# A branch projection by seven half-size products, with its right factors formed one stage earlier

## The chip, the cores and the metric

The kernel runs on one core of a Trainium2 chip. The metric is the device time of one execution in microseconds (us). The profile names the engines PE (TensorE matmul), PEld (its weight loads), DVE (VectorE), ACT (ScalarE), POOL (GpSimd) and SP (SyncE, which here only issues DMAs). L751 is line 751 of the kernel.

## The reference

One encoder layer is applied to two request groups, 256 and 512 tokens, together 768 tokens of width 1024. Three token mixers (an S5 scan, differential attention, cross-attention) each give an output of 1024 channels. What matters here is how they are merged:

```python
branches = jnp.stack([s5_out, diff_out.astype(x.dtype), mem_out.astype(x.dtype)], axis=2)
br = jnp.einsum('blnc,ncd->blnd', branches, w_branch[li])
gates = jax.nn.sigmoid((gl + b_gate[li]).astype(F32)).reshape(Bsz, L, N_BRANCH, D_MODEL)
merged = jnp.sum(gates * br.astype(F32), axis=2).astype(x.dtype)
x = x + merged @ w_out[li]
h2 = rmsnorm(x, ffn_norm_g[li])
g, up = jnp.split(h2 @ w_gate_up[li], 2, axis=-1)
x = x + (jax.nn.silu(g) * up) @ w_down[li]
```

So each branch is a product of a 1024x1024 weight with 1024x768 activations, scaled by a sigmoid gate and summed.

## The kernel before

Activations of all 768 tokens lie with channels on the partitions: a tile of 128 x 8 x 768 holds all 1024 channels. A float32 product is done as three products (`mm3`, L748 to L753): each operand is split into a high part (an ACT copy that rounds) and a low part (a DVE subtraction), and high x high, high x low and low x high are added up in PSUM. `split_evac` (L739) makes such a pair from a source.

Weights stream through `WStream` (L504): SP loads half chunks of 128x1024 into three raw buffers, ACT writes the high part (L595) and DVE the low part (L601) into four buffer pairs. `get()` (L613) hands out a chunk of 256 output columns and first has the splits of the next chunk issued. For the gate and up weights of the FFN the kind is "w": POOL forms four sums of the chunk's quarters (`_split_w`, L561; L572, L573, L577, L579), and ACT and DVE split seven factors of 128x512 (`_factor`, L547; L557, L558). `block` (L1458) then multiplies by Strassen's method in Winograd's form: seven products with half the inner size, half the output rows and half the tokens (384) instead of eight, each four k-steps of `mm3`. The right factors (B11 to B22, T1 to T4) are made once by `right_factors` (L1693).

The three branches go in the order 2, then the GLU of the S5 path, then 0, then 1 (the last branch). `branch` (L1505) takes four chunks of 256 output columns; for each of the two row blocks m of a chunk it loads the gate row from DRAM on POOL's queue (L1513, two buffers), takes its tanh on ACT (L1514), and for the segments of 256 and 512 tokens does eight k-steps of `mm3` into one of three PSUM banks (`psd`). `merge` scales by the gate on DVE (L1520, reads PSUM) and adds to `merged` on DVE (L1523). In the last branch the finished row is split at once into MG (ACT L1554, DVE L1555), the left operand of the output projection. The input of the last branch, `br_scr`, is loaded on POOL's queue row by row (`load_pair`, L1561, two buffers shared under the tag `brr`) and split during branch 0 into the pair Xd (L742, L743). The residual rows x1 are loaded on POOL's queue in the second chunk of branch 0 (L1616). After the last branch come the output projection (`out_rows`, L1633, five PSUM banks), which adds into x1 (L1643), the norm, and the FFN.

Tiles of a pool rotate: a new tile waits until the one that held its buffer has been read. Within an engine, instructions are issued in an order that the framework fixes at build time from its own timeline; `keep_in_program_order` pins an instruction behind everything written before it on its engine.

Of the kernel before, what the change touches and what calls it, by code (L numbers as in the profile page):

```python
# [8 lines left out]
F32 = mybir.dt.float32  # L9
F32R = mybir.dt.float32r  # L10
# [493 lines left out]
class WStream:  # L504
# [53 lines left out]
        self.nc.vector.tensor_tensor(out=f(lo), in0=src, in1=f(hi).bitcast(F32), op=ALU.subtract)  # L558
        self.parts.setdefault(i, {})[key] = f(hi), f(lo)

    def _split_w(self, i, h):  # L561
        gt = self.nc.gpsimd.tensor_tensor
        add, sub = ALU.add, ALU.subtract
        view = lambda t: t.rearrange("p (k m c) -> p m k c", k=4, m=2)
        new = lambda k: self.sums.tile([128, 4, 128], F32, name=f"ws{i}{k}", tag="ws")
        if h == 0:
            return
        a1, a2 = view(self.raw.pop(2 * i)), view(self.raw.pop(2 * i + 1))
        A11, A21, A12, A22 = a1[:, 0], a1[:, 1], a2[:, 0], a2[:, 1]
        self._factor(i, "A11", A11)  # L570
        s1, s2, s3, s4 = (new(k) for k in range(4))
        gt(out=s1, in0=A21, in1=A22, op=add)  # L572
        gt(out=s2, in0=s1, in1=A11, op=sub)  # L573
        self._factor(i, "A12", A12)
        self._factor(i, "S2", s2)
        self._factor(i, "S1", s1)
        gt(out=s3, in0=A11, in1=A21, op=sub)  # L577
        self._factor(i, "S3", s3)
        gt(out=s4, in0=A12, in1=s2, op=sub)  # L579
        self._factor(i, "S4", s4)  # L580
        self._factor(i, "A22", A22)

    def _split(self):
        i, h = divmod(self.n_split, 2)
        self.n_split += 1
        kind = self.src[i][3]
        if kind == "w":
            return self._split_w(i, h)
# [6 lines left out]
        self.nc.scalar.activation(hi, r, AF.Copy)  # L595
# [5 lines left out]
        self.sub.tensor_tensor(out=lo, in0=r, in1=hi.bitcast(F32), op=ALU.subtract)  # L601
# [11 lines left out]
    def get(self, ahead=True):  # L613
        i = self.next
        self.next += 1
        if ahead:
            self.ahead(i + 1)
        _, kk, cols, kind = self.src[i]
        p = self.parts.pop(i)
        if kind == "w":  # L620
            return p
        k2 = kk // 2
        at = lambda t, k, c0, n: t[:, cols * (k % k2) + c0 : cols * (k % k2) + c0 + n]
        return lambda k, c0, n: tuple(at(t, k, c0, n) for t in p[k // k2])


def hybrid_block(ctx, tc, A, outs, consts):
# [20 lines left out]
    def uid(s):  # L648
        cnt[0] += 1
        return f"{s}_{cnt[0]}"  # L650
# [97 lines left out]
    def mm3(ps, wh, wl, xh, xl, start, stop, more=False):  # L748

        kw = {"skip_group_check": True} if more else {}  # L750
        pe.matmul(ps, wh, xh, start=start, stop=False, **kw)  # L751
        pe.matmul(ps, wh, xl, start=False, stop=False, **kw)  # L752
        pe.matmul(ps, wl, xh, start=False, stop=stop, **kw)  # L753
# [740 lines left out]
    with ExitStack() as c5:  # L1494
# [7 lines left out]
        def pair(pool, nm):  # L1502
            return tuple(pool.tile([128, 8, TOK], F32R, name=uid(nm + w), tag="X" + w) for w in ("hi", "lo"))

        def branch(n_, X, first=False, MG=None, tick=None, hook=None):  # L1505
            for c in range(4):
                if hook:
                    hook(c)
                w = W.get()

                def gate(m):
                    g = gtp.tile([128, TOK], F32, name=uid("glr"), tag="glr")
                    gp.dma_start(g, gl_scr[8 * n_ + 2 * c + m])  # L1513
                    act.activation(g, g, AF.Tanh, scale=0.5)  # L1514
                    return g

                def merge(m, g, ps, c0, n):
                    M = 2 * c + m
                    dst = merged[:, M, c0 : c0 + n] if first else g[:, c0 : c0 + n]
                    v.scalar_tensor_tensor(out=dst, in0=g[:, c0 : c0 + n], scalar=1.0, in1=ps[:, 0:n],  # L1520
                                           op0=add, op1=mul)
                    if not first:
                        v.tensor_tensor(out=merged[:, M, c0 : c0 + n], in0=merged[:, M, c0 : c0 + n],  # L1523
                                        in1=dst, op=add)

                if first and c == 0:

                    gs = [gate(m) for m in range(2)]
                    between = lambda: tick(1.0 / 8)
                    for m in range(2):  # L1530
                        ps = psd("br")
                        dense_fm(ps, w, m, X, 0, 256, between=between)
                        merge(m, gs[m], ps, 0, 256)
                        between()
                    pss = [psd("br") for _ in range(2)]
                    for o in (0, 256):
                        for m in range(2):
                            dense_fm(pss[m][:, o : o + 256], w, m, X, 256 + o, 256, between=between)
                            between()
                    for m in range(2):  # L1540
                        merge(m, gs[m], pss[m], 256, 512)
                    continue
                for m in range(2):
                    M = 2 * c + m
                    g = gate(m)
                    for sg, (c0, n) in enumerate(SEGS):
                        ps = psd("br")
                        between = tick and (lambda: tick((1.0 + sg) / 8))
                        dense_fm(ps, w, m, X, c0, n, between=between)
                        merge(m, g, ps, c0, n)  # L1550
                        if tick:
                            between()
                    if MG:
                        act.activation(MG[0][:, M], merged[:, M], AF.Copy, scale=0.5)  # L1554
                        v.scalar_tensor_tensor(out=MG[1][:, M], in0=merged[:, M], scalar=0.5,  # L1555
                                               in1=MG[0][:, M].bitcast(F32), op0=mul, op1=sub)

# [14 lines left out]
        def tail(c):  # L1572
            if c != 3:
                return
            dat.drain()
            dctx.close()
            xp = x1ctx.enter_context(tc.tile_pool(name="x1", bufs=1))
            L["x1"] = [xp.tile([128, 1024], F32, name=f"x1_{t}") for t in range(TILES)]
# [6 lines left out]
        x1, XB, Z = L["x1"], L["XB"], L["Z"]  # L1585
        S = rows_pair("s5o")
        for c in range(4):
            w = W.get()
# [7 lines left out]
            for m in range(2):  # L1596
# [352 lines left out]
```

## Time and profile before

| what | us |
|---|---|
| median of 3 runs (lowest, highest) | 1745.99 (1744.87, 1746.82) |
| the profiled execution | 1746.11 |
| its span | 1744.3 |
| branch 0, first to last product | 1052.9 to 1119.9 |
| last branch, first to last product | 1120.1 to 1186.6 |
| output projection, first to last product | 1186.9 to 1253.7 |
| FFN gate blocks by seven products, first to last start | 1291.7 to 1568 |

Times in the trace count from the start of the span. A matmul's recorded duration is longer than its distance from the next one, since matmuls are pipelined, so rates are taken from starts. A group of instructions is shown as line, engine, operation, output<-input, shapes and count, then durations or busy time, and the idle time of the engine just before with what ended it. The granted TensorE clock was 1.00 in the stretches looked at.

### The profile page before, as it was taken

How to read it: one execution, taken by the hardware profiler on the slowest of the kernel's cores; microseconds unless marked ns; L12 is line 12 of the kernel's file. 1: busy time of each engine (PE TensorE's matmuls, PEld its weight loads, DVE VectorE, ACT ScalarE, POOL GpSimd, SP SyncE). 2: the span in 40 equal slices, each digit the busy share in tenths (PEclk: the TensorE clock that was granted, in tenths of full speed). 3: DMA queues.
4: the chain of work that ended last, by engine and by line, in shares of the span. 5: the costliest groups of instructions: out<-in, count | busy, mean ns of one | idle time of the engine just before them, and what ended most of it. 6: DMA issues, size and time to landing. Idle time of an engine off the chain costs nothing.

```text
span 1744.3 us, 29493 instructions
## 1 busy us (share of the span) xinstructions
PE 1731.5 (99%) x11236; PEld 1606.4 (92%) x11236; DVE 1262.6 (72%) x2353; ACT 889.4 (51%) x1868; POOL 270.1 (15%) x288
## 2 busy tenths in 40 slices
PE   9999999999999999999999999999999999999999
PEld 9999988999999999999989888888889999998887
DVE  7665749699999778887886445453598777776775
ACT  7444543776767346877775434232343333334443
POOL 0000000000000100111010002000036555541130
PEclk9999999999999999999999999999999999999999
DMA  8222736755566453745653437331312323238973
GB/s 271 74 85 91 125 120 134 187 126 141 145 158 159 122 145 93 169 91 155 169 160 106 133 116 247 118 118 61 90 62 91 109 91 109 91 110 290 252 158 96
DMA packets 209214, 234.11 MB, mean 134 GB/s; under 512 B 57832, under 2 KB 173296, under 8 KB 209072
## 3 DMA queue, kind: packets, MB, share of 16 engines
q1 hardware_dynamic: 182160, 167.49, 31.9%
q0 software_dynamic: 17440, 58.34, 15.5%
q10 hardware_dynamic: 9472, 6.39, 1.3%
q8 instruction: 89, 1.46, 0.4%
q14 instruction: 53, 0.43, 0.1%
HBM read 165.78 MB, written 41.22 MB: 119 GB/s over the span
## 4 chain that ended last, share of the span: by engine, by line
PE 96%; DVE 1%; ACT 1%; DMA 1%; issue 0%; SPq 0%; ACTq 0%; DVEq 0%
PE gl L751 4%; PE gl L753 4%; PE gl L752 4%; PE br L751 4%; PE br L752 4%; PE br L753 4%; PE gate L751 3%; PE gate L752 3%; PE up L752 3%; PE gate L753 3%; PE up L751 3%; PE up L753 3%; PE dn L753 3%; PE dn L751 3%; PE dn L752 3%; PE qk L751 3%
## 5 line engine op out<-in xcount | busy, mean ns | idle before, releaser
L595 ACT ACTIVATE wh<-wr 128x1024 fp32r<-128x1024 f32 x124 | 140.4, 1133 | 62.6 <-PE br L752 27.8
L601 DVE TENSOR_TENSOR wl<-wr,wh 128x1024 fp32r<-128x1024 f32 x82 | 108.5, 1324 | 80.8 <-ACT wh L595 79.0
L751 PE MATMUL gl<-H,wh 128*128 128x256 f32 (+1 forms) x384 | 132.2, 344 | 0.0
L753 PE MATMUL gl<-H,wl 128*128 128x256 f32 (+1 forms) x384 | 129.0, 336 | 0.0
L752 PE MATMUL gl<-H,wh 128*128 128x256 f32 (+1 forms) x384 | 128.7, 335 | 0.0
L599 POOL DMA_DIRECT2D wl<-wr x42 | 36.6, 872 | 506.1 <-ACT wl L598 486.8
L751 PE MATMUL qk<-wh,H 128*128 128x256 f32 x384 | 108.1, 282 | 0.0
L752 PE MATMUL qk<-wl,H 128*128 128x256 f32 x384 | 107.8, 281 | 0.0
L753 PE MATMUL qk<-wh,H 128*128 128x256 f32 x384 | 107.1, 279 | 0.0
L752 PE MATMUL dn<-wld,dxh 128*128 128x512 f32 x231 | 89.6, 389 | 0.0
L751 PE MATMUL dn<-whd,dxh 128*128 128x512 f32 x231 | 89.6, 389 | 0.0
L753 PE MATMUL dn<-whd,dxl 128*128 128x512 f32 x231 | 88.9, 389 | 0.0
L753 PEld LDWEIGHTS gl<-H,wl 128*128 128x128 f32 x384 | 72.0, 188 | 8.1
L752 PEld LDWEIGHTS gl<-H,wh 128*128 128x128 f32 x384 | 72.3, 188 | 7.2
L751 PEld LDWEIGHTS gl<-H,wh 128*128 128x128 f32 x384 | 72.3, 188 | 6.8
L557 ACT ACTIVATE wh_S<-ws 128x512 fp32r<-128x512 f32 x70 | 41.1, 625 | 65.2 <-PE up L752 36.8
L753 PEld LDWEIGHTS qk<-wh,H 128*128 128x128 f32 x384 | 72.4, 188 | 0.6
L751 PEld LDWEIGHTS qk<-wh,H 128*128 128x128 f32 x384 | 72.4, 188 | 0.6
L752 PEld LDWEIGHTS qk<-wl,H 128*128 128x128 f32 x384 | 72.3, 188 | 0.5
L558 DVE TENSOR_TENSOR wl_S<-ws,wh_S 128x512 fp32r<-128x512 f32 x70 | 57.9, 851 | 15.9 <-ACT wh_S L557 15.9
L1292 DVE TENSOR_REDUCE nm<-sc 128x1 f32<-128x512 f32 (+1 forms) x96 | 56.6, 596 | 17.6 <-PE sc L1287 16.8
L1294 ACT ACTIVATE p<-sc,nm 128x512 f32<-128x512 f32 (+1 forms) x96 | 58.8, 615 | 14.1 <-DVE nm L1292 13.6
(477 smaller groups left out, 6004.2 us busy)
## 6 DMA issues: line engine op xcount, KB each, us to landing
wr<-in_w_in_dram SPq DMA_DIRECT2D x48, 512.0 KB, 4.9
wr<-in_w_gate_up_dram SPq DMA_DIRECT2D x44, 512.0 KB, 3.6
wl<-wr POOLq DMA_DIRECT2D x42, 512.0 KB, 5.4
wr<-in_w_branch_dram SPq DMA_DIRECT2D x24, 512.0 KB, 4.8
glr<-gl_scr POOLq DMA_DIRECT2D x24, 384.0 KB, 4.0
hid_scr<-fa SPq DMA_DIRECT2D x11, 768.0 KB, 6.5
wr<-in_w_mem_kv_dram SPq DMA_DIRECT2D x16, 512.0 KB, 4.2
wr<-in_w_in_dram SPq DMA_DIRECT2D x32, 256.0 KB, 3.8
```

The source lines that it names most:

```text
L557: self.nc.scalar.activation(f(hi), src, AF.Copy)
L558: self.nc.vector.tensor_tensor(out=f(lo), in0=src, in1=f(hi).bitcast(F32), op=ALU.subtract)
L595: self.nc.scalar.activation(hi, r, AF.Copy)
L599: self.nc.gpsimd.dma_start(lo, r.bitcast(F32R), accum_op=ALU.add)
L601: self.sub.tensor_tensor(out=lo, in0=r, in1=hi.bitcast(F32), op=ALU.subtract)
L751: pe.matmul(ps, wh, xh, start=start, stop=False, **kw)
L752: pe.matmul(ps, wh, xl, start=False, stop=False, **kw)
L753: pe.matmul(ps, wl, xh, start=False, stop=stop, **kw)
L1292: v.tensor_reduce(out=nm[:, m : m + 1], in_=ps, axis=AX.X, op=ALU.max, negate=True)
L1294: act.activation(pm[:, 0:n], ps, AF.Exp, bias=nm[:, m : m + 1], accum_out=s1s[:, tt : tt + 1] if m == 0 else s2)
```

## The change

The last branch is done by seven products a chunk, with the weight kind "w2": as "w", with one buffer fewer for the sums (the fourth is formed in place of the second). Before branch 0 is written, the four row pairs of `br_scr` (rows k and k+4) are loaded and the right factors formed: B11, B22, B21, T1, T3 and T2 are split at once (ACT and DVE), their differences are taken on DVE, and T4 is kept unsplit. Six of the factors lie in the buffers of the Z pair and in the memory of x1, whose loads therefore move behind the last branch; T4's pair lies in the last two rows of MG, which is why the last chunk does A22 T4 before S4 B22.

In a chunk, products add onto banks already in use: S2 T2 and S3 T3 onto the bank of A11 B11 (`chain`), S4 B22 onto that of S1 T1 (`p5`), each after ACT has copied out what the bank held (c11, c12, c22). Four additions from PSUM are left on DVE. Both gate rows of a chunk are loaded at its start, with the two buffers as before. `merge` scales a whole row of 768 in SBUF on DVE, adds it to `merged` on POOL for the first row of the chunk and on DVE for the second, and splits it into MG.

```diff
-    def _split_w(self, i, h):
+    def _split_w(self, i, h, inplace=False):
...
-        s1, s2, s3, s4 = (new(k) for k in range(4))
+        s1, s2 = new(0), new(1)
+        if not inplace:
+            s3, s4 = new(2), new(3)
         gt(out=s1, in0=A21, in1=A22, op=add)
         gt(out=s2, in0=s1, in1=A11, op=sub)
         self._factor(i, "A12", A12)
         self._factor(i, "S2", s2)
         self._factor(i, "S1", s1)
+        if inplace:
+            s3, s4 = new(2), s2
         gt(out=s3, in0=A11, in1=A21, op=sub)
         self._factor(i, "S3", s3)
         gt(out=s4, in0=A12, in1=s2, op=sub)
...
-            W.add(cols(nme, 256 * c), 8, 256)
+            W.add(cols(nme, 256 * c), 8, 256, "w2" if nme == "w_branch1" else None)
...
-        Xd = pair(XB, "xd")
-        load_pair(Xd, br_scr)
-
-        def rows_in(c):
-            if c == 1:
-                for t in range(TILES):
-                    tc.keep_in_program_order(gp.dma_start(x1[t], xs[t]))
-
-        branch(0, S, hook=rows_in)
+        fctx = c5.enter_context(ExitStack())
+        W.sums = fctx.enter_context(tc.tile_pool(name="wsumb", bufs=2))
+        t4p = fctx.enter_context(tc.tile_pool(name="t4raw", bufs=1))
+        t4 = t4p.tile([128, 4, HT], F32, name="t4")
...
+        for k in range(4):
+            r0, r1 = (stg.tile([128, TOK], F32, name=uid("brr"), tag="brr") for _ in range(2))
+            gp.dma_start(r0, br_scr[k])
+            gp.dma_start(r1, br_scr[k + 4])
+            (b11, b12), (b21, b22) = ((r[:, h1], r[:, h2]) for r in (r0, r1))
+            put = lambda n_, src: split_evac(RB[n_][0][:, k], RB[n_][1][:, k], src)
+            put("B11", b11)
+            put("B22", b22)
+            put("B21", b21)
+            v.tensor_tensor(out=b11, in0=b12, in1=b11, op=sub)
+            v.tensor_tensor(out=b12, in0=b22, in1=b12, op=sub)
+            v.tensor_tensor(out=b22, in0=b22, in1=b11, op=sub)
+            v.tensor_tensor(out=t4[:, k], in0=b21, in1=b22, op=sub)
+            put("T1", b11)
+            put("T3", b12)
+            put("T2", b22)
+
+        branch(0, S)
         MG = rows_pair("mgd", 0)
-        branch(1, Xd, MG=MG)
+        RB["T4"] = tuple(t[:, 6:8].rearrange("p a (b t) -> p (a b) t", b=2) for t in MG)
+
+        def branch7(n_):
+            for c in range(4):
+                w = W.get()
+                if c == 0:
+                    for k in range(4):
+                        split_evac(RB["T4"][0][:, k], RB["T4"][1][:, k], t4[:, k])
+                gs = []
+                for m in range(2):
+                    g = gtp.tile([128, TOK], F32, name=uid("glr"), tag="glr")
+                    gp.dma_start(g, gl_scr[8 * n_ + 2 * c + m])
+                    act.activation(g, g, AF.Tanh, scale=0.5)
+                    gs.append(g)
+                cs = [stg.tile([128, TOK], F32, name=uid("bs"), tag="brr") for _ in range(2)]
+                (c11, c12), (c21, c22) = ((t[:, h1], t[:, h2]) for t in cs)
+                chain = env.psb("brc")[:, 0:HT]
...
+                def plus(o, ps):
+                    v.tensor_tensor(out=o, in0=o, in1=ps, op=add)
+
+                def merge(m):
+                    M = 2 * c + m
+                    v.scalar_tensor_tensor(out=cs[m], in0=gs[m], scalar=1.0, in1=cs[m], op0=add, op1=mul)
+                    (v if m else gp).tensor_tensor(out=merged[:, M], in0=merged[:, M], in1=cs[m], op=add)
+                    act.activation(MG[0][:, M], merged[:, M], AF.Copy, scale=0.5)
+                    v.scalar_tensor_tensor(out=MG[1][:, M], in0=merged[:, M], scalar=0.5,
+                                           in1=MG[0][:, M].bitcast(F32), op0=mul, op1=sub)
+
+                act.activation(c11, prod("A11", "B11", chain), AF.Copy)
+                plus(c11, prod("A12", "B21"))
+                act.activation(c12, prod("S2", "T2", chain, False), AF.Copy)
+                p5 = prod("S1", "T1")
+                act.activation(c22, p5, AF.Copy)
+                prod("S3", "T3", chain, False)
+                plus(c22, chain)
+                act.activation(c21, chain, AF.Copy)
+                if c < 3:
+                    plus(c12, prod("S4", "B22", p5, False))
+                    merge(0)
+                    plus(c21, prod("A22", "T4"))
+                    merge(1)
+                else:
+                    plus(c21, prod("A22", "T4"))
+                    merge(1)
+                    plus(c12, prod("S4", "B22", p5, False))
+                    merge(0)
+
+        branch7(1)
+        fctx.close()
+        x1t = xp.tile([128, TILES, 1024], F32, name="x1", tag="x1")
+        x1 = [x1t[:, t] for t in range(TILES)]
+        for t in range(TILES):
+            tc.keep_in_program_order(gp.dma_start(x1[t], xs[t]))
```

`prod(l, r, ps, start)` does the four k-steps of `mm3` on the given bank, or on a new one of the three.

More of the change, by code (lines that the diff above doesn't have):

```diff
@@ L586, in _split @@
         kind = self.src[i][3]
-        if kind == "w":
-            return self._split_w(i, h)
+        if kind in ("w", "w2"):
+            return self._split_w(i, h, kind == "w2")
         hi, lo = self.tiles(f"{i}_{h}")
@@ L619, in get @@
         p = self.parts.pop(i)
-        if kind == "w":
+        if kind in ("w", "w2"):
             return p
@@ L1577, in tail @@
             xp = x1ctx.enter_context(tc.tile_pool(name="x1", bufs=1))
-            L["x1"] = [xp.tile([128, 1024], F32, name=f"x1_{t}") for t in range(TILES)]
+            L["x1"] = xp
             L["XB"] = xbctx.enter_context(tc.tile_pool(name="XB", bufs=1))
@@ new lines, in hybrid_block @@
+        t4p = fctx.enter_context(tc.tile_pool(name="t4raw", bufs=1))
+        t4 = t4p.tile([128, 4, HT], F32, name="t4")
+        quarters = lambda t: [t[:, 2 * j : 2 * j + 2].rearrange("p a (b t) -> p (a b) t", b=2) for j in range(4)]
+        ra, rb = (XB.tile([128, 8, TOK], F32R, name="r" + n_, tag=tg) for n_, tg in (("a", "Xhi"), ("b", "Xlo")))
+        rc = xp.tile([128, 8, TOK], F32R, name="rc", tag="x1")
+        RB = {}
+        for t, ns in ((ra, ("B11", "B21")), (rb, ("B22", "T1")), (rc, ("T2", "T3"))):
+            q = quarters(t)
+            for j, n_ in enumerate(ns):
+                RB[n_] = q[2 * j], q[2 * j + 1]
@@ new lines, in hybrid_block, with prod @@
+        branch(0, S)
+        MG = rows_pair("mgd", 0)
+        RB["T4"] = tuple(t[:, 6:8].rearrange("p a (b t) -> p (a b) t", b=2) for t in MG)
[14 more added lines that the diff above has]
+                chain = env.psb("brc")[:, 0:HT]
+                def prod(l, r, ps=None, start=True):
+                    if ps is None:
+                        ps = psd("br")[:, 0:HT]
+                    (wh, wl), (xh, xl) = w[l], RB[r]
+                    for k in range(4):
+                        mm3(ps, wh[:, k], wl[:, k], xh[:, k], xl[:, k], start and k == 0, k == 3, not start)
+                    return ps
+                def plus(o, ps):
[25 more added lines that the diff above has]
+                    merge(0)
```

3 lines of the change are left out of this document (2 added, 1 removed).

## The prediction

> **What bounds the kernel now.** I read the page first: busy shares and the chain that ended last.
>
> ```profile
> span 1744.3 us, 29493 instructions
> PE 1731.5 (99%) x11236; PEld 1606.4 (92%) x11236; DVE 1262.6 (72%) x2353; ACT 889.4 (51%) x1868; POOL 270.1 (15%) x288
> PE 96%; DVE 1%; ACT 1%; DMA 1%; issue 0%; SPq 0%; ACTq 0%; DVEq 0%
> ```
>
> PE is on the path nearly everywhere, so products taken away are time taken away unless PE then waits. Next came the busy times by stretch (length, PE, PEld, DVE, ACT, POOL, clock, DMA) for branch 0, for the last branch, and for two blocks of the FFN, where seven half-size products are already in use; then the waits of PE between 1052 and 1190 us. That view has one row; between 1290 and 1580 us it has none.
>
> ```profile
> 1052.70:1119.90 67.20, 66.18 (x385) 58.07 (x384) 33.58 (x48) 22.86 (x27) 11.23 (x21) 1.00 0.59 198
> 1119.90:1186.60 66.70, 66.70 (x385) 59.06 (x384) 33.62 (x48) 19.99 (x22) 3.76 (x7) 1.00 0.33 105
> 1335.10:1364.30 29.20, 29.20 (x170) 29.20 (x169) 21.78 (x33) 10.84 (x21) 16.52 (x13) 1.00 0.32 99
> PE br L751 <- DVE glr L1520: 1.0, 1, 1.0
> ```
>
> The last branch runs PE without a gap, with DVE half idle and POOL nearly empty. The FFN runs PE without a gap as well, but on 75% DVE and 57% POOL. The change moves the last branch towards that mix.
>
> **Products.** First and last start of groups of products, with min/median/max of one in ns:
>
> ```profile
> L751 PE MATMUL br<-xdhi,wh x128: 277/336/397, 1120.1 to 1186.2; 128*128 128x256 f32 x64, 128*128 128x512 f32 x64
> L753 PE MATMUL br<-xdhi,wl x128: 282/336/390, 1120.4 to 1186.6; 128*128 128x256 f32 x64, 128*128 128x512 f32 x64
> L751 PE MATMUL gate<-fhi,wh_A x120: 333/334/347, 1291.7 to 1567.8; 128*128 128x384 f32 x120
> L751 PE MATMUL up<-fhi,wh_A x80: 333/334/335, 1306.3 to 1572.0; 128*128 128x384 f32 x80
> ```
>
> Before: 384 products from 1120.1 to 1186.6, 0.174 us apart, 96 a chunk, 16.7 us. After: 7 x 4 x 3 = 84 of width 384. One FFN block is just that, 1291.7 to 1306.3: 14.6 us, 2.09 us for each group of twelve. Four chunks: 58.4 instead of 66.7, **-8.3 us**. That is all the change can give.
>
> **What stands around them.** Durations (ns: min/median/max, or busy us and mean):
>
> ```profile
> L558 DVE TENSOR_TENSOR wl_S<-ws,wh_S x70: 677/692/1780, 1290.5 to 1567.1; 128x512 fp32r<-128x512 f32 x70
> L572 POOL TENSOR_TENSOR ws<-wr,wr x20: 1277/1288/2690, 1264.4 to 1549.0; 128x512 f32<-128x512 f32 x20
> L1436 POOL TENSOR_TENSOR fa<-fa,fs x36: 1012/1456/1472, 1315.1 to 1556.6; 128x384 f32<-128x384 f32 x36
> L1472 DVE TENSOR_TENSOR fs<-fs,gate x70: 540/547/556, 1300.0 to 1568.8; 128x384 f32<-128x384 f32 x70
> L1432 DVE SCALAR_TENSOR_TENSOR fa<-ft,fs x40: 543/559/1644, 1304.6 to 1570.0; 128x384 f32<-128x384 f32 x40
> L743 DVE TENSOR_TENSOR xdlo<-brr,xdhi 128x768 fp32r<-128x768 f32 x8 | 7.6, 954 | 5.4 <-ACT xdhi L742 5.3
> L601 DVE TENSOR_TENSOR wl<-wr,wh 128x1024 fp32r<-128x1024 f32 x16 | 19.6, 1222 | 23.0 <-ACT wh L595 23.0
> L1478 ACT ACTIVATE fs<-gate x10: 492/493/495, 1294.0 to 1556.7; 128x384 f32<-128x384 f32 x10
> L1554 ACT ACTIVATE mgd<-merged 128x768 fp32r<-128x768 f32 x7 | 5.9, 846 | 12.4 <-DVE merged L1523 12.4
> L557 ACT ACTIVATE wh_S<-ws x70: 613/632/635, 1286.7 to 1566.4; 128x512 fp32r<-128x512 f32 x70
> ```
>
> DVE, a chunk that also forms the next one's factors: 7 low parts at 0.68, 5 row operations of width 768 at 0.95 (two scalings by the gate, one add, two MG low parts): 9.5 us with both inputs in SBUF; then 4 additions from PSUM at 0.55, 2.2 us. POOL: four sums at 1.28, and one add of width 768; 384 take 1.01 and 512 take 1.28, so about 1.82: 6.9 us. ACT: 7 x 0.63, 2 tanh and 2 MG rows at 0.85, 4 copies at 0.49: 9.8 us. Each fits in 14.6 alone. Together they need not:
>
> ```profile
> 1333.69 1.49 POOL L573 TENSOR_TENSOR ws<-ws,wr 128x512 f32<-128x512 f32 x1
> 1334.42 1.32 DVE L558 TENSOR_TENSOR wl_S<-ws,wh_S 128x512 fp32r<-128x512 f32 x1
> 1347.40 1.30 POOL L573 TENSOR_TENSOR ws<-ws,wr 128x512 f32<-128x512 f32 x1 [0.90 <-DVE wl_S L558]
> 1347.17 1.01 DVE L1472 TENSOR_TENSOR fs<-fs,up 128x384 f32<-128x384 f32 x2
> ```
>
> POOL's sum ends at 1335.18 and DVE's 0.68 us subtraction at 1335.74, as if it had only begun at 1335.1. The two additions that read PSUM, under another POOL sum, keep their 0.55 (1.01 for two, so neighbours overlap by 0.08 in the records). If all two-SBUF work and POOL's take turns, a chunk needs 9.5 + 6.9 = 16.4 us, or 15.5 less twelve overlaps of 0.08, against 14.6 of PE: at least 0.9 over in each of chunks 0 to 2, which form factors for the next. The FFN, counted the same way, needs 14 x 0.68 + 4 x 0.56 + 8 x 1.28 + 4 x 1.01 = 26.0 in 29.2, and PE does not wait there. The last branch is past that line; an add moved to POOL frees DVE for nothing while DVE must wait for it.
>
> [...]
>
> **The loop through the gate rows.** In the old branch no PE instruction waits for a recent ACT result. In the new one three do in each chunk: S2T2, S3T3 and S4B22 add onto a bank that ACT must have copied out, with one group (2.09 us) as cover. ACT is in order, and the tanh of the second gate row waits for a load that POOL issues only when the previous chunk's scaling has freed the buffer. The load, from the old branch:
>
> ```profile
> 1137.74 0.69 DVE L1523 TENSOR_TENSOR merged<-merged,glr 128x512 f32<-128x512 f32 x1
> 1138.95 0.54 POOL L1513 DMA_DIRECT2D glr<-gl_scr  x1 [7.80 <-DVE merged L1523]
> 1143.03 0.85 ACT L1514 ACTIVATE glr<-glr 128x768 f32<-128x768 f32 x1 [3.72 <-DMA glr<-gl_scr]
> ```
>
> From DVE's end (1138.43) to the tanh: 4.6 us. If the tanh stands ahead of the c12 copy on ACT, a loop closes: S3T3, S4B22, A22T4 (6.3), PSUM addition 0.55, scaling 0.95, load 4.6, tanh 0.85, copy 0.49, next S3T3: 13.7 us, 0.9 under the chunk. Delay on DVE and POOL beyond 0.9 reaches PE. Usual company: one low part (0.68), one MG low part (0.95), one POOL sum in the way (1.28): 2.9; and of two further POOL sums ahead of the load (2.56) I take 1.0. So 3.9 - 0.9 = 3.0 us in each of chunks 1 to 3, **+9.0**. Bounds: 0, as in the FFN, to 3 x 4.6 = 13.8. [...]
>
> **Edges.** Chunk 0: when branch 0 ends, ACT has four factor copies (2.5) and four T4 copies (2.0) ahead of the c11 copy, which ends near 5.0; S2T2 is due at 4.2: **+1.0**, bounds 0 and 3.
>
> Branch 0: per row pair six splits and four differences on DVE, 10 x 0.55, 22 us against 8 x 0.95 = 7.6, and 4.8 instead of 2.4 for the first factors: 33.6 becomes 50 of 67 us. It fits, but DVE is in order, and merges already queue behind these rows:
>
> ```profile
> 1062.96 1.89 DVE L743 TENSOR_TENSOR xdlo<-brr,xdhi 128x768 fp32r<-128x768 f32 x2 [5.02 <-ACT xdhi L742]
> 1064.77 1.01 DVE L1520 SCALAR_TENSOR_TENSOR glr<-glr,br 128x256 f32<-128x256 f32 x2
> 1065.24 0.50 PE L751 MATMUL br<-s5o,wh 128*128 128x512 f32 x1 [1.02 <-DVE glr L1520]
> ```
>
> DVE stood 5 us at a load, the merges behind it kept three PSUM banks, and PE lost 1.0. A group is now 5.5 us long; but six x1 loads leave that stretch. **+1.0**, bounds -1 and +5.
>
> End of the branch (last br product, last MG low part; PE count in 20 us of out-projection; the x1 load):
>
> ```profile
> 1186.63 0.39 PE L753 MATMUL br<-xdhi,wl 128*128 128x512 f32 x1
> 1189.52 0.95 DVE L1555 SCALAR_TENSOR_TENSOR mgd<-merged,mgd 128x768 fp32r<-128x768 f32 x1
> 1200.00:1220.00 20.00, 20.00 (x90) 16.58 (x89) 5.74 (x7) 6.17 (x12) 0.00 (x0) 1.00 0.17 50
> x<-in_x_sample_dram POOLq DMA_DIRECT2D x4, 512.0 KB, 9.1
> ```
>
> The last row is ready 3.5 us after the last product. Now it passes addition, scaling, POOL's add, ACT, DVE: 0.55 + 0.95 + 1.82 + 0.85 + 0.95 = 5.1, and 0.5 for POOL's start. The out-projection (0.222 us a product, 2.7 a group of twelve) reads it after two groups, 5.3: **+1.0**, bounds 0 and 2.5. The x1 loads, now behind that add, land some 13 us after the end instead of long before; the first sum wants x1 at 8, but five banks, a new one every 5.3 us, cover 16. Nothing; without that cover, 5.
>
> Sum: -8.3 + 9.0 + 1.0 + 1.0 + 1.0 = +3.7. The profiled execution took 1746.11 us (span 1744.3), 0.1 over the median of 1745.99: **1749.8 us**. The bounds add up to 1736.8 and 1762.1.
>
> **Rivals.** (1) Faster: the loop never closes, because ACT has the copies ahead of the tanh or the delay stays under 0.9 us. [...] Price: half the edges, 1.5, so -6.8: 1739.3. [...] (3) The tanh ahead even of the c11 copy: the loop takes in S2 and S1 too, 13.7 + 4.2 = 17.9, and with 2.0 of delay it is 5.3 over, 15.8 in three chunks: -8.3 + 15.8 + 3.0 = +10.5, 1756.6. For it: the tanh is issued first in the chunk; against it: its load lands some 5 us in, after c11 is ready.
>
> **How the numbers follow.** Forecast 0.38, (1) 0.30, (2) 0.19, (3) 0.13. A measurement tells 0.2% (3.5 us) from no change. Faster: (1) and 0.06 of (2), 0.36. Same: 0.13 of (2), 0.12 of the forecast's near side, 0.25. Slower: 0.26 + 0.13 = 0.39. The range, 1738.5 to 1758.0, leaves out a clean gain below it and the far half of (3); the forecast's own is 1746 to 1755.
>
> **What would show it.** Right: in PE's waits, S2, S3 or S4 groups of the last branch released by ACT's copies, tanh just ahead of them with idle time put down to the gate load; chunks 1 to 3 near 17.6 us; a short wait of PE on mgd; POOL adds over 1.82. Wrong: chunks of 14.6 with no wait (rival 1), waits released by DVE or POOL factors alone (rival 2), or a longer branch 0.

## The result, and the profile after

The changed kernel takes 1742.64 us (median of 13 runs, 1740.81 to 1744.48) against 1746.82 for the kernel before beside it: ratio 0.9977, 95% interval 0.9968 to 0.9985. The prediction said 1749.8 and put most on slower. The time lies in its range, on the other side of no change. Ratios here and below are not ratios of the medians and can stand a little off them.

The profiled execution took 1743.06 us, 3.05 less than the one of before. First the page, then the stretches of branch 0, of the last branch and of two cells inside it (length, busy time of PE, PEld, DVE, ACT, POOL, granted clock, DMA share, GB/s), then the waits of PE between 1040 and 1200 us.

```profile
span 1741.3 us, 29531 instructions
PE 1726.6 (99%) x11188; PEld 1608.1 (92%) x11188; DVE 1300.5 (75%) x2405; ACT 908.6 (52%) x1924; POOL 302.5 (17%) x308
```

```profile
1053.90:1120.70 66.80, 66.80 (x385) 58.71 (x384) 46.69 (x82) 27.27 (x45) 14.81 (x19) 1.00 0.47 144
1120.70:1183.80 63.10, 60.65 (x338) 59.77 (x337) 51.58 (x62) 33.92 (x60) 26.93 (x22) 0.97 0.38 119
1156.51:1159.92 3.41, 1.29 (x8) 1.18 (x8) 3.41 (x4) 1.21 (x2) 3.39 (x3) 1.00 0.44 140
1159.92:1163.33 3.41, 3.41 (x12) 3.41 (x11) 3.41 (x5) 1.48 (x2) 0.59 (x2) 0.50 0.49 154
```

```profile
PE brc L757 <- DVE wl_A L558: 2.1, 1, 2.1
PE brc L755 <- ACT bs L1683: 0.3, 1, 0.3
```

In branch 0 DVE went from 33.6 to 46.7 us busy and PE has no wait left; the stretch is 66.8 us instead of 67.2. The last branch is 63.1 us long instead of 66.8. With 336 products at the FFN's pace it would be 58.4, so of the 8.3 us that the products give, 3.7 arrived. The missing 4.6 lie mostly in one place: a wait of 2.1 us on a low part, and behind it 3.4 us in which the granted clock was 0.50 and PE got through 12 products. The groups of twelve there took 5.0 us instead of 2.1 and, for six products of the next, 1.9 instead of 1.0: 3.8 us together, 2.3 for the wait (counted from start to start) and 1.5 for the slow products behind it. A c11 copy costs 0.3, the rest is spread over groups that took 2.2 instead of 2.09.

The place itself, with POOL, DVE and PE in order of time (start, us, engine, line, idle before and its releaser):

```profile
1154.24 2.22 POOL L1678 TENSOR_TENSOR merged<-merged,bs 128x768 f32<-128x768 f32 x1 [2.34 <-DVE bs L1677]
1155.15 3.54 DVE L558 TENSOR_TENSOR wl_A<-wr,wh_A 128x512 fp32r<-128x512 f32 x2
1156.42 1.71 POOL L574 TENSOR_TENSOR ws<-wr,wr 128x512 f32<-128x512 f32 x1
1158.74 0.44 PE L757 MATMUL brc<-ra,wl_A 128*128 128x384 f32 x1 [2.12 <-DVE wl_A L558]
```

Two low parts that take 0.68 each alone took 3.54 under POOL's add and, right behind it, POOL's sum. The product that waited is the first low one of chunk 3's A11 B11: the build had placed it ahead of what was left of chunk 2. This is the turn-taking that the prediction read from the FFN's rows. VectorE is held in the same way elsewhere (a low part of the same size took 2.33 from 1137.84 on, under POOL's add of chunk 0), but only in this one spot did PE wait for it.

### The profile page after: what moved, and what is told of

The parts are those of the page before. It is cut to its first block, busy times and chain, and to the rows that moved or that the text cites. A ratio compares the mean times of both kernels' runs of the same rounds, so it can differ in the third digit from the quotient of the medians.

```text
span 1741.3 us, 29531 instructions
## 1 busy us (share of the span) xinstructions
PE 1726.6 (99%) x11188; PEld 1608.1 (92%) x11188; DVE 1300.5 (75%) x2405; ACT 908.6 (52%) x1924; POOL 302.5 (17%) x308
## 4 chain that ended last, share of the span: by engine, by line
PE 95%; DVE 2%; ACT 1%; issue 0%; DMA 0%; POOL 0%; SPq 0%; ACTq 0%; DVEq 0%
PE gl L755 4%; PE gl L756 4%; PE gl L757 4%; PE gate L755 3%; PE gate L756 3%; PE up L756 3%; PE gate L757 3%; PE up L755 3%; PE up L757 3%; PE dn L757 3%; PE dn L755 3%; PE dn L756 3%; PE br L755 3%; PE br L757 3%; PE br L756 3%; PE qk L755 3%
## 5 line engine op out<-in xcount | busy, mean ns | idle before, releaser
L599 ACT ACTIVATE wh<-wr 128x1024 fp32r<-128x1024 f32 x116 | 131.9, 1138 | 52.3 <-PE br L756 13.3
L605 DVE TENSOR_TENSOR wl<-wr,wh 128x1024 fp32r<-128x1024 f32 x74 | 99.2, 1342 | 63.5 <-ACT wh L599 61.7
L558 DVE TENSOR_TENSOR wl_S<-ws,wh_S 128x512 fp32r<-128x512 f32 x84 | 70.7, 863 | 26.2 <-ACT wh_S L557 26.2
L557 ACT ACTIVATE wh_S<-ws 128x512 fp32r<-128x512 f32 x84 | 49.5, 625 | 73.5 <-PE up L756 36.6
```

Source lines behind the costliest of these rows:

```text
L557: self.nc.scalar.activation(f(hi), src, AF.Copy)
```

## The experiments

Ratios are to the kernel before run beside them. Two groups of theories were in question: what holds PE up in the new branch (the loop through the gate rows, POOL's adds, POOL's sums), and why the loop did not cost what was forecast.

**All adds on DVE, and all on POOL.**

```diff
-                    (v if m else gp).tensor_tensor(out=merged[:, M], ...
+                    v.tensor_tensor(out=merged[:, M], ...      # none on POOL
+                    gp.tensor_tensor(out=merged[:, M], ...     # all on POOL
```

> All eight merged rows are added on VectorE, none on POOL. Theory port (the one 2.1 us wait of PE in the last branch comes from a VectorE low part held up by POOL's 768-wide add and the sum behind it): without that add the wait shrinks below 0.7 us or goes, although VectorE has 0.95 us a chunk more to do; no slow clock after it; 1738.5 to 1740.5 us. Rival load (VectorE is simply too full in that stretch): the wait grows to 3 us or more, 1744 to 1747 us.

> All eight merged rows are added on POOL. Theory port: POOL reads SBUF 8.8 us a chunk and VectorE's two-SBUF work 8.5 us, 17.3 against 14.6 of PE; two or more waits of PE for low parts, each with a slow clock behind it; 1744 to 1748 us. Rival load: VectorE has 0.95 us a chunk less, the wait shrinks, 1739 to 1741 us.

Measured with no add on POOL 1740.16 us (ratio 0.9965, 0.9952 to 0.9979); with all eight 1745.39 (0.9993, 0.9984 to 1.0001). With the change's four at 1742.64 the steps are 2.5 and 2.8 us: adds moved to POOL gained nothing here. The interval of none overlaps that of four, which touches that of all; only none and all are clear of each other. Nor are the steps the adds' alone, because the build ordered the products anew in each run: at least 65 (none) and 97 (all) of the last branch's 336 places hold another product than in the change.

With all eight, the waits that theory port expects did not come. One low part cost 0.9; the larger waits are for ScalarE's copies, the largest of the out-projection for the last c21 copy (L1690), with 3.4 us at clock 0.50 from 1.3 us behind it on:

```profile
PE wo L755 <- ACT bs L1690: 2.1, 1, 2.1
PE brc L755 <- ACT bs L1683: 1.0, 1, 1.0
PE brc L757 <- DVE wl_A L558: 0.9, 1, 0.9
```

With none, the time lies where theory port had it, but the wait on the low part stays:

```profile
PE brc L757 <- DVE wl_A L558: 2.0, 1, 2.0
1154.14 1.68 POOL L574 TENSOR_TENSOR ws<-wr,wr 128x512 f32<-128x512 f32 x1 [4.00 <-DVE wl_S L558]
1154.58 2.05 DVE L1677 SCALAR_TENSOR_TENSOR bs<-glr,bs 128x768 f32<-128x768 f32 x1
1155.89 1.86 POOL L575 TENSOR_TENSOR ws<-ws,wr 128x512 f32<-128x512 f32 x1
1156.55 2.35 DVE L558 TENSOR_TENSOR wl_A<-wr,wh_A 128x512 fp32r<-128x512 f32 x2
```

Here POOL's two sums stretch DVE's scaling from 0.95 to 2.05 and the two low parts to 2.35. So the add is not the only POOL work that holds DVE; the sums do it alone. In this run the granted clock stayed at 1.00, in the change's it did not: of the 1.9 us by which the last branch is shorter here (61.1 against 63.0), 1.5 are the slow products.

**POOL's sums left out.** The last branch splits quarters of the weight instead of S1 to S4.

```diff
-        gt(out=s1, in0=A21, in1=A22, op=add)
-        gt(out=s2, in0=s1, in1=A11, op=sub)
+        if not inplace:
+            gt(out=s1, in0=A21, in1=A22, op=add)
+            gt(out=s2, in0=s1, in1=A11, op=sub)
+        else:
+            s1, s2 = A21, A11
...
+            s3, s4 = A21, A12
...
```

> Left out: POOL's four sums a chunk of the last branch's weights; the quarters A21, A11, A21 and A12 stand in for S1 to S4, so that part of the computation is changed, with the same number of factors and products. Theory port: VectorE does the same work and is held up only by the one add a chunk, no wait of PE over 0.5 us in the last branch, 1738 to 1739.5 us. Rival load: VectorE's load is unchanged, the wait of about 2 us stays, 1741.5 to 1743.5 us.

Measured 1741.18 (0.9969, 0.9958 to 0.9981), with POOL's adds as in the change. The wait on the low part is gone, and others have come in its stead:

```profile
PE wo L760 <- ACT bs L1695: 1.7, 1, 1.7
PE br L760 <- DVE bs L1678: 1.0, 1, 1.0
```

Without the sums that wait does not come (the build's order of the products is another one here, too). Taking them away is worth 1.5 us, within the intervals: the out-projection's first bank now waits for the last c21 copy.

**POOL's adds in the old branch.** The second part of the change alone, in the kernel before.

```diff
+                        e = gp if MG and m == 0 else v
-                        v.tensor_tensor(out=merged[:, M, c0 : c0 + n], ...
+                        e.tensor_tensor(out=merged[:, M, c0 : c0 + n], ...
```

> The kernel before with the change's second part alone: in the last branch the adds of the upper row of each chunk (eight, in two column stretches a row) on POOL; products, factors and weights as before. Theory A (POOL's adds cost time by what they hold up inside a branch of seven products: low parts of the sums, ScalarE's copies in order behind the add): in the old branch, where no product waits for ScalarE or for POOL's sums and PE was busy in 66.80 of 66.80 us, nothing, ratio 0.999 to 1.001; at most one wait on a low part under 1 us. Theory B (a POOL add costs some 0.6 us by itself, 2.5 us for four rows as between the runs with no, half and all adds on POOL): 1748 to 1749, ratio 1.0015.

Measured 1745.98 us (1.0002, 0.9993 to 1.0011), and PE has no wait in the branch. So four rows added on POOL have no price of their own that this run could show, 1.9 us at the interval's end. That they cost in the new branch because POOL's sums and short covers stand around them is argued from the waits above.

**The products in written order.** In the change the build places products itself, and it had moved S1 T1, A22 T4 and part of the next chunk's A11 B11 between the products that wait for copies. Here each product is pinned in the order of the source.

```diff
-                        mm3(ps, wh[:, k], wl[:, k], xh[:, k], xl[:, k], start and k == 0, k == 3, not start)
+                        pin_ = tc.keep_in_program_order
+                        pin_(pe.matmul(ps, wh[:, k], xh[:, k], ...))
+                        pin_(pe.matmul(ps, wh[:, k], xl[:, k], ...))
+                        pin_(pe.matmul(ps, wl[:, k], xh[:, k], ...))
```

> The products of the last branch are issued in the order in which they are written. Theory of the prediction (the loop of gate load, tanh, c12 copy and S3T3 closes when no product is moved ahead): waits of PE for ACT's copies in every chunk, chunks 1 to 3 of about 17 us, 1748 to 1751 us. Rival (the order of the products matters little, the copies are out in time): no wait for a copy over 0.5 us, 1741 to 1744 us.

Measured 1743.41 (0.9981, 0.9972 to 0.9990), so no different from the change in total. But the waits are other ones: L1687 is the c11 copy, L1689 the c12 copy.

```profile
PE brc L1671 <- ACT bs L1687: 2.0, 2, 1.1
PE brc L1671 <- ACT bs L1689: 1.7, 3, 0.7
```

```profile
1136.09 2.30 POOL L1682 TENSOR_TENSOR merged<-merged,bs 128x768 f32<-128x768 f32 x1
1138.42 0.84 ACT L1683 ACTIVATE mgd<-merged 128x768 fp32r<-128x768 f32 x1 [0.64 <-POOL merged L1682]
1139.17 0.47 ACT L1687 ACTIVATE bs<-brc 128x384 f32<-128x384 f32 x1
1141.80 0.85 ACT L1683 ACTIVATE mgd<-merged 128x768 fp32r<-128x768 f32 x1 [2.15 <-DVE merged L1682]
1142.55 0.83 ACT L1658 ACTIVATE glr<-glr 128x768 f32<-128x768 f32 x1
1144.32 0.47 ACT L1689 ACTIVATE bs<-brc 128x384 f32<-128x384 f32 x1
1144.84 0.44 PE L1671 MATMUL brc<-rc,wh_S 128*128 128x384 f32 x1 [0.71 <-ACT bs L1689]
1174.99 0.85 ACT L1658 ACTIVATE glr<-glr 128x768 f32<-128x768 f32 x1 [1.31 <-DMA glr<-gl_scr]
```

The wait on the c12 copy comes once in each of chunks 1 to 3, as the prediction has it, but with 0.7, 0.7 and 0.3 us. A tanh (L1658) stands ahead of the copy each time, yet only in chunk 3 (the last row) is ScalarE's idle time before it put down to the gate load. In chunks 1 and 2 ScalarE last idled 2.15 us at the lower row's MG copy, for DVE's add; the tanh and two factor copies followed without a gap, and then the c12 copy. The larger waits, 0.9 and 1.1, are ones the prediction did not have: the c11 copy stands behind the upper row's MG copy, and that behind POOL's add.

**Written order, adds on DVE.** Both edits together.

> Products in the written order, and all merged rows added on VectorE. In the written order alone PE waited 2.0 us for c11 copies (behind an MG copy that waits for POOL's add) and 1.7 us for c12 copies (behind the tanh of a gate row). Theory (each of the two has its own cause): the c11 waits go with POOL's add, the c12 waits stay, 1.7 us or so; no wait for a low part, since A11 B11 of the next chunk is not moved ahead; 1740.5 to 1741.5 us. Rival (ACT's copies are late because ACT and VectorE are full): both kinds stay, 1743 to 1744 us.

Measured 1740.58 (0.9973, 0.9964 to 0.9982). The waits fall from 3.7 to 1.6 us:

```profile
PE brc L1671 <- ACT bs L1687: 1.3, 1, 1.3
PE brc L1671 <- ACT bs L1689: 0.3, 1, 0.3
```

Neither theory fits the waits: a c11 wait stays, in chunk 1, where the MG copy ahead of it now waits for DVE's add (1.72 us under one of POOL's sums, 0.94 alone), and the c12 waits shrink as well. With the adds on DVE the time falls again, by 2.8 us of the medians or, by the ratios, 1.4, within the intervals. This and the version with the adds on DVE alone are the fastest kernels here that compute the whole layer, 4.7 and 6.1 us under the kernel before by their ratios, where the change is 4.0 under it.

**More gate buffers, in written order.** Chunks 1 and 3 take their gate rows from the memory of the raw T4, so that no load waits for the scaling of the chunk before; POOL's adds stay.

```diff
+                g2 = t4p.tile([128, 2, TOK], F32, name=uid("glt"), tag="t4") if c % 2 else None
-                    g = gtp.tile([128, TOK], F32, name=uid("glr"), tag="glr")
+                    g = g2[:, m] if c % 2 else gtp.tile([128, TOK], F32, name=uid("glr"), tag="glr")
```

> Products in the written order, POOL adds as in the changed kernel, and two more gate-row buffers (in T4's memory, chunks 1 and 3), so that gate rows can be loaded a chunk ahead. Theory (the loop through the gate rows is what makes the c12 copies late): the c12 waits (1.7 us in the written order) go, the c11 waits (2.0 us) stay: 1741.3 to 1742.3 us. Rival (the tanh is only passing by): no change, 1743 to 1744 us.

Measured 1747.32 (1.0009, 0.9999 to 1.0018), 4 to 5 us more than without the buffers. The waits on the c12 copy are gone. In chunk 2 the lower row's MG copy waits for DVE's add as before (2.15 us), but the tanh no longer stands between it and the c12 copy, so its place in ScalarE's queue accounts for that wait (0.7 us, a tanh 0.75 from start to start). In their place one of 5.2 us stands ahead of the c11 copy's reader:

```profile
1138.84 2.25 POOL L1683 TENSOR_TENSOR merged<-merged,bs 128x768 f32<-128x768 f32 x1
1141.93 1.58 ACT L1684 ACTIVATE mgd<-merged 128x768 fp32r<-128x768 f32 x2 [4.22 <-DVE merged L1683]
1143.41 0.47 ACT L1688 ACTIVATE bs<-brc 128x384 f32<-128x384 f32 x1
1143.94 0.69 PE L1672 MATMUL brc<-rc,wh_A 128*128 128x384 f32 x1 [5.16 <-ACT bs L1688]
```

ACT idles 4.2 us at the head of two MG copies while the c11 copy, ready, stands behind them; the add that it waits for took DVE 2.55 us, most of it under POOL's add. In the run without the buffers one MG copy stood there, not two. The 3.4 us behind the wait ran at clock 0.50.

**More gate buffers, the build's order, adds on DVE.**

> All adds on VectorE and the two more gate-row buffers, products in the order that the framework picks. Theory (the 2.0 us wait for a low part comes from POOL's two sums holding the port while the next chunk's A11 B11 has been moved ahead): it stays as long as that product is ahead; 1739.5 to 1740.8 us. Rival (the move ahead came from the late tanh and copies): with the tanh out of the way it goes, 1737.5 to 1738.8 us.

Measured 1745.11 (0.9996, 0.9987 to 1.0004), 5 us more than without the buffers. Waits of 2.9 us of the out-projection on the last c21 copy, 1.0 on an addition from PSUM and 1.0 on a c22 copy replace the one on the low part, with 6.8 us at half clock around the first. The buffers changed the order that the build chose on every engine, so this run doesn't price the loop; it shows no gain from freeing the rows.

**x1 loaded late, in the kernel before.** The x1 loads stand behind the last branch; the rest is as before.

```diff
-                for t in range(TILES):
-                    tc.keep_in_program_order(gp.dma_start(x1[t], xs[t]))
...
+        for t in range(TILES):
+            tc.keep_in_program_order(gp.dma_start(x1[t], xs[t]))
```

> The kernel before with one part of the change: the six x1 loads issued behind the last branch. Theory (the 1.0 us wait of PE at the start of branch 0 came from the row loads held up by the x1 loads): the wait goes and nothing waits for x1 later: 1.0 us faster, 1745.5 to 1746.2 us. Rival (late x1 rows hold up the out-projection): a wait of 2 us or more behind the last branch, 1747.5 to 1750 us.

Measured 1745.75 us (1.0002, 0.9993 to 1.0010). The 1.0 us wait in branch 0 is gone from the trace, no wait for x1 has come, and the span was 1743.0 against 1744.3, 0.8 of it ahead of the first branch; the total can't tell it. So the wait in branch 0 goes with the loads that left, and the factors' work in the change costs PE next to nothing there (66.6 us from first to last start, against 66.4 in this run).

**Another order of the products.** Two groups of cover for each copy instead of one, adds on DVE, then the same with the change's adds on POOL.

```diff
                 act.activation(c11, prod("A11", "B11", chain), AF.Copy)
+                p5 = prod("S1", "T1")
+                act.activation(c22, p5, AF.Copy)
                 plus(c11, prod("A12", "B21"))
                 act.activation(c12, prod("S2", "T2", chain, False), AF.Copy)
-                p5 = prod("S1", "T1")
-                act.activation(c22, p5, AF.Copy)
+                plus(c12, prod("S4", "B22", p5, False))
+                p4 = prod("A22", "T4")
+                merge(0)
                 prod("S3", "T3", chain, False)
...
```

> Written order, all adds on VectorE, and the seven products of a chunk put in the order A11 B11, S1 T1, A12 B21, S2 T2, S4 B22, A22 T4, S3 T3, so that each ScalarE copy of the PSUM chain has two groups of products (4.2 us) ahead of the next product that writes the same bank, where the order of the change gave it one (2.1 us). Theory A (with the order fixed, what is left to lose are the chain's copies, because one group covers a copy of 0.47 us only while nothing stands ahead of it on ScalarE): the copy waits of 1.6 us of the run in written order with VectorE adds go, none over 0.3 us is left, the last branch falls from 61.7 us to 59 to 60, the time to 1738 to 1739.5. Theory B (the wait only moves: to the low parts at the next chunk's start, or to the out-projection's bank, because the chunk's last copy and add now come later): a wait of 1 to 2 us on VectorE's low part or on the last copy, time 1740 to 1742.

> The same order of products as the run before it, with the upper row's add of each chunk on POOL as in the change. Theory A (POOL's add costs by what stands behind it on ScalarE and VectorE, and cover of two groups swallows that): within 1 us of the run before it. Theory B (POOL's adds cost by holding VectorE up, whatever the order): a wait on a low part or on a copy of 1 to 2 us that the run before it doesn't have, 1.5 to 3 us more, 1740 to 1742.

Measured 1749.72 (1.0014, 1.0005 to 1.0022) and 1749.06 (1.0015, 1.0006 to 1.0023): slower than the kernel before. The first one's waits:

```profile
PE br L1671 <- ACT bs L1689: 3.5, 2, 2.8
PE wo L755 <- DVE bs L1677: 3.0, 1, 3.0
PE brc L1671 <- ACT bs L1687: 0.4, 1, 0.4
```

Theory A failed. The c11 wait shrank to 0.4, but the two scalings, adds and MG rows of a chunk now come in one lump at its end, so the c22 copy (L1689) of the next chunk stands behind an MG copy, and the out-projection behind the last additions. With that lump POOL's adds make no difference either way (the second one's waits are 4.4 us on c22 copies and 3.0 of the out-projection). Part of the loss is clock: in the first one's profile 3.4 us at 0.50 follow the wait of 2.8 and another 3.4 begin at the end of the wait of 3.0. Its one execution with a mean clock of 1.000 took 1744.07, the other eleven, at 0.996 to 0.998, 1746.83 to 1750.85.

**Idle stretches of TensorE of four lengths.** The half clock of the change's run was new. Ahead of each chunk of the old last branch, whose products are pinned, TensorE is made to wait for a chain of ScalarE copies. There is one execution, 1764.16 us.

```diff
+                    tc.keep_in_program_order(pe.matmul(gb[:, 0:128], env.ident, env.ident, start=True, stop=True))
+                    act.activation(jk[:, 512:640], gb[:, 0:128], AF.Copy)
+                    for _ in range((1, 2, 3, 4)[c]):
+                        act.activation(jk[:, 0:512], jk[:, 512:513].to_broadcast([128, 512]), AF.Copy)
+                    tc.keep_in_program_order(pe.matmul(gb[:, 0:128], jk[:, 0:128], env.ident, start=True, stop=True))
```

> The kernel before, with its last branch's products in written order, and ahead of each of the last branch's four chunks a short TensorE product, a chain of one, two, three or four ScalarE copies of 512 columns, and a product that needs the chain's end: idle stretches of TensorE of four lengths (about 1.2 to 3 us; the trace gives them). Theory A (idle time of TensorE over about 2.05 us is followed by some 3 us at half the granted clock, as in the runs so far, where 2.0 us was not and 2.1 us was): full clock after the stretches below 2.0 us, about 3.3 us at 0.50 after those above 2.1 us. Theory B (the half clock came from the work around the waits, such as weights changed at every product, and not from the length of the wait): full clock after all four, or half after all.

The products behind the four stretches, with the wait ahead of each:

```profile
1121.31 0.49 PE L1524 MATMUL gap<-ident,gapj 128*128 128x128 f32 x2 [1.52 <-ACT gapj L1523]
1141.47 0.49 PE L1524 MATMUL gap<-ident,gapj 128*128 128x128 f32 x2 [2.77 <-ACT gapj L1523]
1162.29 0.49 PE L1524 MATMUL gap<-ident,gapj 128*128 128x128 f32 x2 [3.43 <-ACT gapj L1523]
1185.29 0.80 PE L1524 MATMUL gap<-ident,gapj 128*128 128x128 f32 x2 [4.09 <-ACT gapj L1523]
```

After 1.52 and 2.77 the clock stayed at 1.00; after 3.43 it was 0.50 for 3.4 us, after 4.09 for 6.8. Both theories fall: 2.77 did nothing here while 2.12 did in the change. What both runs have in common is in the last section.

## Why the prediction was wrong

**Products, -8.3: right.** 28 groups of twelve, each 2.08 to 2.09 us where nothing holds them.

**The loop through the gate rows, +9.0: the step that failed.** In the change no product waits for the c12 copy. The pieces of the loop are there (gate load on POOL, tanh, c12 copy and the next S3 T3 in the change's trace, for chunk 1):

```profile
1133.75 0.33 PE L755 MATMUL brc<-rc,wh_S 128*128 128x384 f32 x1
1143.16 0.55 POOL L1657 DMA_DIRECT2D glr<-gl_scr  x1 [1.73 <-DVE bs L1677]
1145.71 0.85 ACT L1679 ACTIVATE mgd<-merged 128x768 fp32r<-128x768 f32 x1 [1.95 <-DVE merged L1678]
1146.83 0.84 ACT L1658 ACTIVATE glr<-glr 128x768 f32<-128x768 f32 x1
1148.60 0.48 ACT L1685 ACTIVATE bs<-brc 128x384 f32<-128x384 f32 x1
1150.04 0.33 PE L755 MATMUL brc<-rc,wh_S 128*128 128x384 f32 x1
```

From S3 T3 of chunk 0 to the end of chunk 1's c12 copy are 15.3 us, against 17.6 (13.7 and 3.9 of delay) in the prediction and 14.6 free. So the 3.0 a chunk was mis-sized: 0.7 by these rows, and 0.7, 0.7 and 0.3 in the run with the products pinned. The path was in part another one, too. The last idle time of ScalarE ahead of the c12 copy is put down to DVE's add of chunk 0's lower row (1.95 us, at the MG copy) and not to the gate load, and two factor copies (1.1 us) stand between the tanh and the c12 copy, which the prediction's sum leaves out. Pinned, only chunk 3 has idle time at the gate load. What holds the c12 copy is all that stands ahead of it on ScalarE; the tanh is one piece of it. The two guesses that made the delay large, a sum of all usual company on top of each other and the upper half between 0 and 13.8, had no row behind them that showed them together.

And even the 0.7 did not reach PE, because the build's order had put other products (all of chunk 2's first group) ahead of that S3 T3, so that the two S3 T3 are 16.3 us apart with PE at work between them. The prediction took the written order for the executed one. That slip decided where the waits fell, not the total: pinned, the kernel takes 1743.41. There the waits and what follows them make the last branch 63.8 us, 5.4 over its products, with more than half of the waiting ahead of readers of the c11 copy, and no slow clock.

**DVE's and POOL's turns: seen, wrong in place and weight.** The prediction's count (DVE's and POOL's work over the chunk's 14.6 us) puts 0.9 over in each of three chunks. It came as one wait of 2.1, where POOL's add and sum met two low parts that a moved-up product needed, and, pinned, as 2.0 us behind the c11 copy. Rival (2) of the chances is this count alone: 2.7 in three chunks and the 3.0 of edges, 5.7 beside the products' -8.3, which makes -2.6 and 1743.5. That ended within 1 us of the result (-2.6 within 1.6 of the measured change), but the 3.0 of edges did not occur; in their place stood the 1.5 of half clock. Its number comes near by errors that cancel, which is luck. "Port" is the author's word in the theories for whatever the two engines take turns at. What it is, no run shows: the rows show that DVE's work takes longer while POOL's runs (3.54 instead of 1.36 us, 2.05 instead of 0.95).

**Chunk 0, +1.0, and the end, +1.0: nothing.** No wait of PE in either place. The 0.5 us for POOL's start in the end's sum was the author's estimate, and no run shows it: in the change's trace POOL's last add begins at 1188.21, 0.08 us after the scaling that it waits for.

**Branch 0, +1.0: -0.4.** The bounds of -1 to +5 held it; the reason given for a gain (the x1 loads leave) is what the run with late loads shows.

**x1 behind the branch: nothing, as said.**

The sum: -8.3 + 3.8 (wait and slow products) + 0.8 (the c11 copy and groups of 2.2) - 0.4 (branch 0) = -4.1, with -4.2 between the medians. Between the two profiled executions it is -3.05. The missing 1.0 is work ahead of branch 0, which begins at 1053.9 instead of 1052.9; 0.9 of it is there already where the first branch begins (879.2 against 878.3), ahead of all that the diff touches. It is not the change's: in the fourteen profiles here TensorE, ScalarE and POOL run the same instructions in the same order up to that point (VectorE too, but for a swapped neighbour or two), and it comes anywhere from 877.3 to 880.4 us.

**What stays open.** Which of the waits a given order produces was not foreseen by any theory here: the attempts to free a copy (the buffers, twice, and the spread order) each made a longer wait elsewhere. And the 2.5 us between no and four adds on POOL stand within the intervals; only the 5 us between none and all are clear of them. How much of those is the adds, how much the build's other order and how much half clock is not shown: there is one trace of each, and with the order pinned the step from four to none is 1.4 us by the ratios, within the intervals.

## What to carry to other kernels

Where products must wait for an in-order engine, price the queue ahead of the instruction they wait for (here one MG copy that waits for POOL; with more gate buffers in written order ScalarE idled 4.2 us at an MG copy while a copy that was ready stood behind it), with the order that the build executes, not the written one. Work moved to POOL to relieve DVE need not relieve it: here two low parts took 3.54 us instead of 1.36 beside POOL's add and sum, the kernel with all eight rows on POOL was some 5 us slower than with none, and in a branch where no product depends on that chain four rows cost nothing that could be measured. A chain delay got by adding up usual company is a guess until a row shows the pieces together: 3.0 us a chunk was forecast here, and at most 0.7 came.

## What the runs showed of the hardware

A wait of PE could cost more than its length here (in the change's run 2.3 us for the wait and 1.5 for the slow products behind it), and whether it did went with where it fell. In each profile with slow stretches, they begin and end on a grid of 3.41 us. In slices of 1 us, the run with two groups of cover and DVE adds has them begin here (the clock is the third number from the end):

```profile
908.00:909.00 1.00, 0.76 (x5) 0.78 (x6) 0.94 (x4) 1.00 (x4) 0.00 (x0) 0.72 0.00 0
1147.00:1148.00 1.00, 0.85 (x3) 0.85 (x4) 1.00 (x2) 1.00 (x3) 0.00 (x0) 0.69 0.24 98
1188.00:1189.00 1.00, 0.20 (x1) 0.20 (x2) 1.00 (x3) 0.00 (x0) 1.00 (x3) 0.67 0.63 223
```

A mean of 0.72 is half clock for the last 0.56 of the slice, so the starts are 908.44, 1147.38 and 1188.34: 238.94 and 40.96 apart, 70 and 12 cells of 3.413 us. Cut along the grid, a cell in which PE was busy for less than about half (0.45 or less, see below) was followed by a cell at 0.50. In the change's run this is the cell from 1156.51 shown above (1.29 of 3.41 busy). In the run with four idle stretches, first the cells around 2.77 us of waiting, then those around 3.43:

```profile
1139.95:1143.36 3.41, 1.89 (x16) 1.89 (x17) 1.98 (x2) 1.47 (x3) 0.54 (x1) 1.00 0.82 247
1143.36:1146.77 3.41, 3.41 (x23) 3.03 (x22) 0.84 (x2) 0.84 (x1) 0.00 (x0) 1.00 0.39 150
1156.99:1160.41 3.42, 1.87 (x10) 1.40 (x8) 2.93 (x4) 2.18 (x5) 0.00 (x0) 1.00 0.18 35
1160.41:1163.82 3.41, 1.53 (x13) 1.53 (x14) 1.68 (x2) 1.79 (x3) 0.54 (x1) 1.00 0.85 256
1163.82:1167.23 3.41, 3.41 (x18) 3.31 (x17) 0.23 (x1) 0.84 (x1) 0.00 (x0) 0.50 0.36 136
```

The 2.77 us straddled a boundary, leaving 1.89 us of work in the cell and the clock at 1.00; the 3.43 us left 1.53 in its second cell, and the next ran at 0.50. So a wait of 2.1 us inside one cell was followed by 3.4 us at half clock, and one of 2.8 us across two was not. Over the fourteen profiles, cells with a busy share of 0.45 and less were followed by half clock, and cells with 0.49 and more by full clock, but for one of small products with 0.62 by its records. Three cells at half clock with 0.69 to 0.73 busy were followed by another one. Where the grid lies differs from one execution to the next (the first slow stretch of the last branch began at 1147.38 and at 1147.93 in the two runs with two groups of cover), so, by inference, the same wait need not cost the same each time. One such cell takes 0.001 off the mean clock of a whole execution (half of 3.41 in 1741 us): of the change's thirteen, three at 1.000 took 1740.81 to 1741.94, nine at 0.999 1741.62 to 1743.97 and one at 0.998 1744.48.
